# Norm weights beside the loaded features, squares of x in program order and a ScalarE root at the end, in a four-layer decoder trunk

## The chip, the core and the metric

The kernel runs on one core of a Trainium2 chip. Five engines work side by side: PE (TensorE, matrix products; PEld is its loading of weights), DVE (VectorE), ACT (ScalarE), POOL (GpSimd) and SP (SyncE, which here only issues transfers). Each engine takes its own instructions in order; semaphores order them between engines. DMA transfers are issued from the queues of SP, ACT and POOL. The metric is the device time of one execution in microseconds (us), lower being better.

## The reference, cut to what matters

The reference is a decoder trunk of four layers over 256 rows of width 2048, all in float32. Each layer normalizes x, projects it once into the streams of a mixer, four memory query heads and a SiLU gate, and adds an output projection to x. At the end x is normalized once more.

```python
def _rmsnorm(x, g):
    xf = x.astype(jnp.float32)
    y = xf * lax.rsqrt(jnp.mean(xf * xf, axis=-1, keepdims=True) + EPS)
    return (y * g.astype(jnp.float32)).astype(x.dtype)

mem_n = _rmsnorm(mem, mem_norm)
for i in range(DEPTH):
    h = _rmsnorm(x, norm_in[i])
    ...                                   # mixer i % 3, memory attention on mem_n @ w_mem_kv[i]
    y = jnp.concatenate([self_out, mem_out], axis=-1) * jax.nn.silu(gate)
    x = x + y @ w_out[i]
return _rmsnorm(x, final_norm)
```

## The kernel before, in words

**Products in two parts.** Every large product is made from a high and a low part of both operands: ACT copies a float32 tile into a rounded tile (`wh`, L60), DVE subtracts to get the rest (`wl`, L69), and PE runs three products per pair (L265 to L267 for row-wise products, L285 and L289 for column-wise ones). Weights stream from HBM into the tile `wr` (five buffers) by SP's queue; `wh` and `wl` have three buffers each.

**The opening.** `memory()` projects the normalized memory for all four layers (eight steps, each one row-wise product of 16 weight tiles and two column-wise ones). The memory's features (the transposed memory, laid out on the host) come in four tiles `ft` of four 128x256 pieces each, two pieces to a transfer (L88). `weighted_parts` (L193) multiplies a piece by its norm weight, a column of `gvec`, and splits it into the high part (ACT, L60) and the low part (DVE, L198) of `mT`. `gvec` holds all norm weights that are used by feature; ACT's queue loads it as its first transfer (L78). In the very first product the weight tiles come one by one, and a function `each(k)` (L371), called behind the k-th weight tile's transfer, issues the next features behind odd k. PE runs some small products on a tile of ones (L102) while it waits.

**Features of x.** From the second of the eight steps on, a generator `first_chunk(c)` (L322) is run beside the products, once for each quarter of x's features. It issues two loads of `ft` (L326) and two loads of the rows of x (L112), lets six calls of `other_work` go by, makes the four weighted pieces one a call, and then traces two squares-and-sums of the rows of x (L339, the helper's line is L203), one a call. Behind the last quarter, `finish` turns the eight sums into the row scales. The sums are read only by `finish`.

**Who sets the order.** A planner orders each engine's instructions when the program is built: it plays the program against a model of times and lets what is ready go first, by program order among the ready. `keep_in_program_order(i)` adds one edge: i goes behind the instruction that was traced just before it on the same engine. The weighted copies of ACT and the early transfers carry such edges; the squares of x do not. Small tiles come from pools by width: all `[P, 2]` scratch tiles (`mn`, `sm`, `ms`, `rc`, `sd`, `se`, `sa` of the softmaxes, the temporaries of the row scales, and `warm`, on which ACT runs one Exp at the start) share six buffers, and a buffer is free again when its tile's last use is over.

**The late constants.** `late_constants()` (L114) and `bias_table` (L128) load small constants by POOL's queue at the end of the first memory step: `caus`, `cos`, `sin`, `nsink`, then `oh`, `rb` and `mk`, from which PE makes a bias table (L136).

**The end.** `last_out` (L963) makes the last output projection. Its column groups end one after the other; for each, DVE adds the sums to x (L973), ACT squares and sums the new x (L203), and DVE multiplies x by the final norm weight (L978). `share` (L992) gathers the mean of squares, times -1/2; `rsqrt_of` (L994) takes the root by an integer first guess and three Newton steps, seven small DVE instructions (L997, L1002, L1004); `write` (L1008) scales the row tile by pieces on DVE and ACT and stores them. The second row tile is last: its last 256 columns end the program.

Of the kernel before, what the change touches and what calls it, by code (L numbers as in the profile page):

```python
# [8 lines left out]
F32 = mybir.dt.float32  # L9
# [22 lines left out]
def kernel(ctx: ExitStack, tc: tile.TileContext, a: dict, out: bass.AP,  # L32
# [20 lines left out]
    def f32(ap):  # L53
        return ap.bitcast(F32)
# [23 lines left out]
    tc.keep_in_program_order(nc.scalar.dma_start(gvec, a["l_norms"]))  # L78

    class Features:  # L80

        def __init__(self, src, c):
            self.q = act.tile([P, 4, S], F32, name="ft", tag="pq", bufs=PQ)
            self.src = src[:, 4 * c:4 * c + 4, :]

        def load(self, h):
            tc.keep_in_program_order(
                nc.sync.dma_start(self.q[:, 2 * h:2 * h + 2, :], self.src[:, 2 * h:2 * h + 2, :]))  # L88

    mft = [Features(a["l_mem"], c) for c in range(4)]  # L90
    mft[0].load(0)
# [22 lines left out]
    def late_constants():  # L114
        tc.keep_in_program_order(nc.gpsimd.dma_start(caus, a["c_caus"]))
        tc.keep_in_program_order(nc.gpsimd.dma_start(cos, a["c_cos"].rearrange("(t p) d -> p t d", p=P)))
        tc.keep_in_program_order(nc.gpsimd.dma_start(sin, a["c_sin"].rearrange("(t p) d -> p t d", p=P)))
        sk = a["c_sinks"]
        tc.keep_in_program_order(nc.gpsimd.dma_start(
            nsink, bass.AP(tensor=sk.tensor, offset=sk.offset, ap=[[0, P], [1, 32]])))  # L120
        nc.vector.tensor_scalar(nsink, nsink, -1.0, None, op0=OP.mult)
# [71 lines left out]
    def weighted_parts(dst, src, k, gcol):  # L193


        g = gvec[:, gcol + k:gcol + k + 1]
        copy_act(dst[:, 0, k, :], src[:, k, :], scale=g)
        nc.vector.scalar_tensor_tensor(dst[:, 1, k, :], src[:, k, :], g, f32(dst)[:, 0, k, :],  # L198
                                       op0=OP.mult, op1=OP.subtract)

    def square_sum(col, src):
        junk = tmp("junk")
        return nc.scalar.activation(junk[:, :src.shape[-1]], src, AF.Square, accum_out=col).ins  # L203
# [104 lines left out]
    class Norm:  # L308
# [13 lines left out]
        def first_chunk(self, c):  # L322

            ft = Features(a["l_x"], c)
            for h in range(2):
                ft.load(h)  # L326
            first_rows(c)
            for _ in range(12):
                yield True
            q = act.tile([P, 2, 4, S], F32R, name="xT", tag="xT", bufs=4)  # L330
            self.at.append(q)
            for k in range(4):
                pinned.append(c)
                weighted_parts(q, ft.q, k, 64 + c * 4)
                pinned.pop()
                yield True
                yield True
            for t in range(2):
                square_sum(self.ss[:, t * 4 + c:t * 4 + c + 1], x[t][:, c * 512:(c + 1) * 512])  # L339
                yield True  # L340
                yield True
            if c == 3:
                self.finish()
# [20 lines left out]
    def memory():  # L364
# [6 lines left out]
        def each(k):  # L371

            if k % 2 and k < 15:
                mft[(k + 1) // 4].load((k + 1) // 2 % 2)
            if k == 15:
                tc.keep_in_program_order(nc.sync.dma_start(ident, a["c_ident"]))
                nc.vector.tensor_copy(identr, ident)

        def prepare(k):
            c = k // 4  # L380
            weighted_parts(mT[c], mft[c].q, k % 4, c * 4)
# [581 lines left out]
    def last_out(w, part, y):  # L963
# [7 lines left out]
        def add(c0, n, t, acc, col):  # L971
            xs = x[t][:, c0:c0 + n]
            inst = nc.vector.tensor_add(xs, xs, acc)  # L973
            return inst.ins, square_sum(f4[:, t * 5 + col:t * 5 + col + 1], xs)
# [19 lines left out]
        def rsqrt_of(v):  # L994

            i1 = small("fj", 1, I32)
            nc.vector.tensor_scalar(i1, v.bitcast(I32), -0.5, float(0x5F3759DF - (1 << 22) - (1 << 30)),  # L997
                                    op0=OP.mult, op1=OP.add)
            r = i1.bitcast(F32)
            for it in range(3):  # L1000
                u = small("fu", 1)
                nc.vector.scalar_tensor_tensor(u, r, v, r, op0=OP.mult, op1=OP.mult)  # L1002
                r2 = small("fy", 1)
                inst = nc.vector.scalar_tensor_tensor(r2, u, 1.5, r, op0=OP.add, op1=OP.mult)  # L1004
                r = r2
            return r, inst
# [41 lines left out]
        v0 = small("fv", 1)  # L1048
        share(v0, f4[:, 3:4], early[0])
        r, inst = rsqrt_of(v0)  # L1050
# [6 lines left out]
        v1, v2 = small("fv", 1), small("fv", 1)  # L1057
# [3 lines left out]
        share(v2, f4[:, 9:10], v1)  # L1061
        weigh(nc.vector, 1536 + S, S, 1)
        r, inst = rsqrt_of(v2)
# [97 lines left out]
def _laid_out(inputs):  # L1161

    import numpy as np

    def features(v):
        return np.asarray(v)[0].T.reshape(D // P, P, S).transpose(1, 0, 2)
    norms = np.zeros((P, P), np.float32)
    for name, o in (("mem_norm", 0), ("a_q_norm", 32), ("a_kv_norm", 56), ("norm_in", 64)):
        v = np.asarray(inputs[name]).reshape(-1, P)
        norms[o:o + len(v)] = v  # L1170
    return {"l_x": features(inputs["x"]), "l_mem": features(inputs["mem"]), "l_norms": norms.T}
# [27 lines left out]
```

## Time and profile before

| | |
|---|---|
| median of 3 runs | 2589.91 us (2589.48 to 2590.26) |
| the profiled execution | 2588.94 us, span 2587.2 us, granted TensorE clock 0.999 |
| PE busy | 2573.5 us (99% of the span) |
| DVE, ACT, POOL busy | 1878.8, 1619.6, 86.8 us (73%, 63%, 3%) |
| moved by DMA | 520.02 MB, mean 201 GB/s |

The span runs from the first to the last instruction. In rows of the timeline the first number is the start in us from the span's start, the second the duration; a bracket at the end gives the idle time of the engine before the row and what ended it. "PEq", "SPq" and the like are an engine's sequencer, which issues transfers and waits. In lists of waits, the numbers are the total in us, how often, and the longest. A row of a group gives its count, and behind the bar its busy time in us and the mean of one in ns. In rows of transfers the last number is the time from issue to landing. A product row's duration is modelled, and back-to-back products overlap; the step from one start to the next is the cost of one.

### The profile page before, as it was taken

The page shows a single profiled execution, that of the slowest core. Times are in us where ns is not written, and L with a number is a line of the kernel's source. Part 1 is how long each engine was busy: PE and PEld are TensorE (multiplying, and loading weights), DVE is VectorE, ACT ScalarE, POOL GpSimd, SP SyncE. Part 2 cuts the span into 40 slices and gives each one's busy share as a digit, 9 for nine tenths or more (in the row PEclk, how much of TensorE's full clock was granted, in tenths as well). Part 3 has the DMA queues.
Part 4 walks back from the last instruction along what each step waited for, and adds up shares of the span by engine and source line. Part 5 has one row for each costly group of instructions (what it writes and reads, how often), then busy time and mean ns, then how long its engine had stood idle before and what let it go on. Part 6 is the DMA issues. An engine that isn't in the chain of part 4 may idle for free.

```text
span 2587.2 us, 41766 instructions
## 1 busy us (share of the span) xinstructions
PE 2573.5 (99%) x14050; PEld 2214.7 (86%) x14050; DVE 1878.8 (73%) x4145; ACT 1619.6 (63%) x3446; POOL 86.8 (3%) x159
## 2 busy tenths in 40 slices
PE   9999999999999999999999999999999999999998
PEld 8888898888888888888888888888888888888887
DVE  6666667677776686877778776777778767777666
ACT  6556556556656566667666666676666655665654
POOL 1000000000000010000000000000000000000000
PEclk9999999999999999999999999999999999999999
DMA  9887777666677668566656575555655877666664
GB/s 309 255 260 255 241 215 234 182 169 194 190 201 203 198 214 249 167 202 188 187 166 199 169 224 171 172 175 183 195 156 148 239 205 197 192 192 183 209 176 175
DMA packets 459128, 520.02 MB, mean 201 GB/s; under 512 B 69488, under 2 KB 352640, under 8 KB 457248
## 3 DMA queue, kind: packets, MB, share of 16 engines
q1 hardware_dynamic: 441600, 449.72, 59.0%
q0 software_dynamic: 16736, 66.65, 7.9%
q8 instruction: 110, 1.80, 0.3%
q14 instruction: 106, 0.87, 0.1%
q10 hardware_dynamic: 576, 0.98, 0.1%
HBM read 494.10 MB, written 35.75 MB: 205 GB/s over the span
## 4 chain that ended last, share of the span: by engine, by line
PE 91%; DVE 0%; ACT 0%; issue 0%; ACTq 0%; DVEq 0%
PE acc_g L285 14%; PE acc_g L289 7%; PE acc_wo L265 7%; PE acc_wo L266 7%; PE acc_wo L267 7%; PE acc_mq L285 5%; PE acc_cq L285 3%; PE acc_qn L285 3%; PE acc_mq L289 2%; PE acc_mk L285 2%; PE acc_q L266 2%; PE acc_q L267 2%; PE acc_q L265 2%; PE acc_cq L289 2%; PE acc_qn L289 2%; PE ptp L487 1%
## 5 line engine op out<-in xcount | busy, mean ns | idle before, releaser
L69 DVE TENSOR_TENSOR wl<-wr,wh 128x512 fp32r<-128x512 f32 (+2 forms) x1720 | 1160.8, 678 | 620.1 <-ACT wh L60 599.1
L60 ACT ACTIVATE wh<-wr 128x512 fp32r<-128x512 f32 (+2 forms) x1720 | 1065.2, 621 | 797.7 <-PE acc_g L285 173.4
L285 PE MATMUL acc_g<-xT,wh 128*128 128x512 f32 x1536 | 486.8, 396 | 0.0
L289 PEld LDWEIGHTS acc_g<-xT,wl 128*128 128x128 f32 x1536 | 284.5, 188 | 60.5
L289 PE MATMUL acc_g<-xT,wl 128*128 128x256 f32 x1536 | 310.1, 280 | 0.0
L266 PE MATMUL acc_wo<-wl,y 128*128 128x512 f32 x752 | 297.3, 395 | 0.2 <-DVE wl L69 0.2
L267 PE MATMUL acc_wo<-wh,y 128*128 128x512 f32 x752 | 291.8, 390 | 0.0
L285 PEld LDWEIGHTS acc_g<-xT,wh 128*128 128x128 f32 x1536 | 238.3, 189 | 4.5
L265 PE MATMUL acc_wo<-wh,y 128*128 128x512 f32 x752 | 235.7, 392 | 0.1
L266 PEld LDWEIGHTS acc_wo<-wl,y 128*128 128x128 f32 x752 | 141.3, 188 | 27.7 <-DVE wl L69 0.6
L267 PEld LDWEIGHTS acc_wo<-wh,y 128*128 128x128 f32 x752 | 141.3, 188 | 27.3
L265 PEld LDWEIGHTS acc_wo<-wh,y 128*128 128x128 f32 x752 | 139.3, 188 | 28.7 <-ACT y L60 1.0
L285 PE MATMUL acc_mq<-xT,wh 128*128 128x512 f32 x512 | 161.6, 396 | 0.0
L285 PE MATMUL acc_mk<-mT,wh 128*128 128x512 f32 x512 | 161.5, 396 | 0.0
L1112 DVE TENSOR_TENSOR x<-x,acc_wo 128x512 f32<-128x512 f32 x184 | 121.2, 682 | 4.4 <-PE acc_wo L267 4.3
L285 PE MATMUL acc_qn<-cT,wh 128*128 128x512 f32 x384 | 121.3, 397 | 0.0
L285 PE MATMUL acc_cq<-xT,wh 128*128 128x512 f32 x384 | 120.9, 396 | 0.0
L289 PEld LDWEIGHTS acc_mk<-mT,wl 128*128 128x128 f32 x512 | 96.1, 188 | 22.8 <-DVE wl L69 0.4
L289 PEld LDWEIGHTS acc_mq<-xT,wl 128*128 128x128 f32 x512 | 93.9, 188 | 20.1
L289 PE MATMUL acc_mq<-xT,wl 128*128 128x256 f32 x512 | 103.1, 282 | 0.0
L266 PE MATMUL acc_q<-wl,xT 128*128 128x512 f32 x256 | 101.2, 395 | 0.0
L289 PE MATMUL acc_mk<-mT,wl 128*128 128x256 f32 x512 | 101.1, 278 | 0.0
(325 smaller groups left out, 4340.3 us busy)
## 6 DMA issues: line engine op xcount, KB each, us to landing
wr<-in_w_out_dram SPq DMA_DIRECT2D x188, 512.0 KB, 3.7
wr<-in_w_in_a_dram SPq DMA_DIRECT2D x176, 512.0 KB, 4.1
wr<-in_w_mem_kv_dram SPq DMA_DIRECT2D x120, 512.0 KB, 4.8
wr<-in_w_in_b_dram SPq DMA_DIRECT2D x112, 512.0 KB, 3.7
wr<-in_w_in_c_dram SPq DMA_DIRECT2D x104, 512.0 KB, 3.6
wr<-in_w_uq_dram SPq DMA_DIRECT2D x192, 128.0 KB, 3.1
wr<-in_w_uq_dram SPq DMA_DIRECT2D x48, 256.0 KB, 3.8
tab<-flat POOLq DMA_DIRECT2D x8, 1536.0 KB, 9.4
```

Source lines behind the costliest of these rows:

```text
L60: inst = nc.scalar.activation(o, i, AF.Copy, scale=scale)
L69: nc.vector.tensor_sub(lo, src, f32(hi))
L265: nc.tensor.matmul(acc[t][:, :n], xh, wh[:, :n], start=first, stop=False)
L266: nc.tensor.matmul(acc[t][:, :n], xh, wl[:, :n], start=False, stop=False)
L267: nc.tensor.matmul(acc[t][:, :n], xl, wh[:, :n], start=False, stop=last)
L285: nc.tensor.matmul(acc[j], wh[:, o:o + P], q[:, :, kt % 4, :], start=kt == 0, stop=False)
L289: nc.tensor.matmul(acc[j][:, 0, :], wl[:, o:o + P], q[:, 0, kt % 4, :], start=False, stop=kt == kts - 1)
L487: nc.tensor.transpose(tp[:, i * P:(i + 1) * P], es[b][:, k * P:(k + 1) * P], ident)
L1112: nc.vector.tensor_add(xs, xs, acc[t])
```

## The change

- The host lays out the features with the norm weight of each feature as a 257th column, so the tile `ft` becomes 4 x 257 columns and the weight is read from there; `gvec` no longer holds the memory's weights, and its load moves from the head of ACT's queue to the head of `late_constants` on POOL's.
- The first feature tile's first two pieces come in two transfers: the first alone, the second behind the first weight tile's transfer.
- The squares of x in `first_chunk` are kept in program order.
- `rsqrt_of` takes the root with ACT's Sqrt, DVE's reciprocal and one Newton step. A Sqrt on the tile `warm` is traced ahead of the last column groups.

```diff
     gvec = cst.tile([P, P], F32, name="gvec")
-    tc.keep_in_program_order(nc.scalar.dma_start(gvec, a["l_norms"]))
...
-            self.q = act.tile([P, 4, S], F32, name="ft", tag="pq", bufs=PQ)
+            self.q = act.tile([P, 4, S + 1], F32, name="ft", tag="pq", bufs=PQ)
...
-        def load(self, h):
-            tc.keep_in_program_order(
-                nc.sync.dma_start(self.q[:, 2 * h:2 * h + 2, :], self.src[:, 2 * h:2 * h + 2, :]))
+        def load(self, k0, n=2):
+            tc.keep_in_program_order(nc.sync.dma_start(self.q[:, k0:k0 + n, :], self.src[:, k0:k0 + n, :]))
...
-    mft[0].load(0)
+    mft[0].load(0, 1)
...
     def late_constants():
+        tc.keep_in_program_order(nc.gpsimd.dma_start(gvec, a["l_norms"]))
         tc.keep_in_program_order(nc.gpsimd.dma_start(caus, a["c_caus"]))
...
-    def weighted_parts(dst, src, k, gcol):
-        g = gvec[:, gcol + k:gcol + k + 1]
-        copy_act(dst[:, 0, k, :], src[:, k, :], scale=g)
-        nc.vector.scalar_tensor_tensor(dst[:, 1, k, :], src[:, k, :], g, f32(dst)[:, 0, k, :],
+    def weighted_parts(dst, src, k):
+        g = src[:, k, S:S + 1]
+        copy_act(dst[:, 0, k, :], src[:, k, :S], scale=g)
+        nc.vector.scalar_tensor_tensor(dst[:, 1, k, :], src[:, k, :S], g, f32(dst)[:, 0, k, :],
                                        op0=OP.mult, op1=OP.subtract)
...
             for t in range(2):
-                square_sum(self.ss[:, t * 4 + c:t * 4 + c + 1], x[t][:, c * 512:(c + 1) * 512])
+                tc.keep_in_program_order(
+                    square_sum(self.ss[:, t * 4 + c:t * 4 + c + 1], x[t][:, c * 512:(c + 1) * 512]))
                 yield True
                 yield True
...
         def each(k):
+            if k == 0:
+                mft[0].load(1, 1)
             if k % 2 and k < 15:
-                mft[(k + 1) // 4].load((k + 1) // 2 % 2)
+                mft[(k + 1) // 4].load((k + 1) % 4)
...
-        def rsqrt_of(v):
-            i1 = small("fj", 1, I32)
-            nc.vector.tensor_scalar(i1, v.bitcast(I32), -0.5, float(0x5F3759DF - (1 << 22) - (1 << 30)),
-                                    op0=OP.mult, op1=OP.add)
-            r = i1.bitcast(F32)
-            for it in range(3):
-                u = small("fu", 1)
-                nc.vector.scalar_tensor_tensor(u, r, v, r, op0=OP.mult, op1=OP.mult)
-                r2 = small("fy", 1)
-                inst = nc.vector.scalar_tensor_tensor(r2, u, 1.5, r, op0=OP.add, op1=OP.mult)
-                r = r2
-            return r, inst
+        def rsqrt_of(col, rest):
+            e = small("fd", 1)
+            nc.vector.tensor_scalar(e, rest, -2.0, None, op0=OP.mult)
+            v = small("fv", 1)
+            share(v, col, rest)
+            q = small("fq", 1)
+            nc.scalar.activation(q, col, AF.Sqrt, bias=e, scale=1.0 / D)
+            r = small("fr", 1)
+            nc.vector.reciprocal(r, q)
+            u = small("fu", 1)
+            nc.vector.scalar_tensor_tensor(u, r, v, r, op0=OP.mult, op1=OP.mult)
+            r2 = small("fy", 1)
+            return r2, nc.vector.scalar_tensor_tensor(r2, u, 1.5, r, op0=OP.add, op1=OP.mult)
...
             for t in range(2):
                 add(c * 512, 512, t, acc[t], c)
+
+        tc.keep_in_program_order(nc.scalar.activation(warm, warm, AF.Sqrt))
         acc = [ps.tile([P, 512], F32, name="acc_wo2", tag="acc", bufs=4) for c in range(5)]
...
-        v0 = small("fv", 1)
-        share(v0, f4[:, 3:4], early[0])
-        r, inst = rsqrt_of(v0)
+        r, inst = rsqrt_of(f4[:, 3:4], early[0])
...
-        v1, v2 = small("fv", 1), small("fv", 1)
+        v1 = small("fv", 1)
         share(v1, f4[:, 8:9], early[1])
...
-        share(v2, f4[:, 9:10], v1)
         weigh(nc.vector, 1536 + S, S, 1)
-        r, inst = rsqrt_of(v2)
+        r, inst = rsqrt_of(f4[:, 9:10], v1)
```

More of the change, by code (lines that the diff above doesn't have):

```diff
@@ L202, in square_sum @@
         junk = tmp("junk")
-        return nc.scalar.activation(junk[:, :src.shape[-1]], src, AF.Square, accum_out=col).ins
+        return nc.scalar.activation(junk[:, :src.shape[-1]], src, AF.Square, accum_out=col)
     def stage(w, k0, m, cols, each=None):
@@ L325, in first_chunk @@
             for h in range(2):
-                ft.load(h)
+                ft.load(2 * h)
             first_rows(c)
@@ L333, in first_chunk @@
                 pinned.append(c)
-                weighted_parts(q, ft.q, k, 64 + c * 4)
+                weighted_parts(q, ft.q, k)
                 pinned.pop()
@@ L380, in prepare @@
             c = k // 4
-            weighted_parts(mT[c], mft[c].q, k % 4, c * 4)
+            weighted_parts(mT[c], mft[c].q, k % 4)
         def memory_rows(c):
@@ L973, in add @@
             inst = nc.vector.tensor_add(xs, xs, acc)
-            return inst.ins, square_sum(f4[:, t * 5 + col:t * 5 + col + 1], xs)
+            return inst.ins, square_sum(f4[:, t * 5 + col:t * 5 + col + 1], xs).ins
         def weigh(engine, c0, n, t):
@@ L1163, in _laid_out, with features @@
     import numpy as np
-    def features(v):
-        return np.asarray(v)[0].T.reshape(D // P, P, S).transpose(1, 0, 2)
+    def features(v, g):
+        beside = np.concatenate([np.asarray(v)[0].T, np.asarray(g).reshape(-1)[:D, None]], 1)
+        return beside.reshape(D // P, P, S + 1).transpose(1, 0, 2)
     norms = np.zeros((P, P), np.float32)
-    for name, o in (("mem_norm", 0), ("a_q_norm", 32), ("a_kv_norm", 56), ("norm_in", 64)):
+    for name, o in (("a_q_norm", 32), ("a_kv_norm", 56), ("norm_in", 64)):
         v = np.asarray(inputs[name]).reshape(-1, P)
         norms[o:o + len(v)] = v
-    return {"l_x": features(inputs["x"]), "l_mem": features(inputs["mem"]), "l_norms": norms.T}
+    return {"l_x": features(inputs["x"], inputs["norm_in"]),
+            "l_mem": features(inputs["mem"], inputs["mem_norm"]), "l_norms": norms.T}
 _INS = ["x", "mem", "final_norm", "rel_bias", "w_in_a", "w_uq",
```

## The prediction

> **What bounds it now.** I read the page's head and its chain first, then the list of what PE waited for, then the timeline around each of those waits, and last the end. The chain is the work that ended last, followed back.
>
> ```profile
> span 2587.2 us, 41766 instructions
> ...
> PE 91%; DVE 0%; ACT 0%; issue 0%; ACTq 0%; DVEq 0%
> ```
>
> ```profile
> PE acc_mv L265 <- ACT wh L60: 2.5, 2, 1.2
> PE wu L102 <- DVE ones L98: 1.1, 1, 1.1
> PE o L950 <- DVE pT L69: 0.3, 1, 0.3
> ```
>
> PE is the bound nearly from end to end: in 2587 us its waits for other engines come to two stops of 1.2 us behind ACT's `wh` (the opening, and one later); the warm-up on `ones` lies ahead of the first, and the longest after that is 0.3 us. So an edit pays only where it starts PE earlier, takes the second stop away, or shortens what follows the last product. The change touches all three.
>
> **The opening.** The fences give the timeline, the rate of all transfers in slices of 1 us from 0 to 40 us, and the first transfers.
>
> ```profile
> 4.92 0.51 ACT L60 ACTIVATE mT<-ft,gvec 128x256 fp32r<-128x256 f32 x1 [2.24 <-DMA gvec<-in_l_norms_dram]
> ...
> 5.45 0.63 ACT L60 ACTIVATE wh<-wr 128x512 fp32r<-128x512 f32 x1
> ...
> 6.13 0.73 PE L265 MATMUL acc_mv<-wh,mT 128*128 128x512 f32 x2 [1.24 <-ACT wh L60]
> ...
> 8.18 0.63 ACT L60 ACTIVATE wh<-wr 128x512 fp32r<-128x512 f32 x1 [0.34 <-DMA wr<-in_w_mem_kv_dram]
> ...
> 8.84 0.69 DVE L69 TENSOR_TENSOR wl<-wr,wh 128x512 fp32r<-128x512 f32 x1 [0.48 <-ACT wh L60]
> ...
> 9.71 0.40 PE L266 MATMUL acc_mv<-wl,mT 128*128 128x512 f32 x1
> ```
>
> ```profile
> GB/s 0 29 165 268 348 322 336 332 397 383 397 404 393 389 383 377 385 387 393 375 372 352 371 372 359 365 359 366 369 359 353 352 339 345 343 309 343 202 110 362
> ```
>
> ```profile
> ft<-in_l_mem_dram SPq DMA_DIRECT2D x1, 256.0 KB, 4.0
> wr<-in_w_mem_kv_dram SPq DMA_DIRECT2D x1, 256.0 KB, 4.2
> gvec<-in_l_norms_dram ACTq DMA_DIRECT2D x1, 64.0 KB, 4.2
> ```
>
> `gvec`, issued at 0.73, lands at 4.9 and ends ACT's wait; the features (issued at 0.74) lay there at 4.7. But the first weight tile, issued at 1.17, lands only at 5.4, just as ACT is through with its first piece, so taking the wait for `gvec` away gives nothing by itself: the weight tile would be late next. What helps is that less lies ahead of that tile: 128 KB of features (the second piece now follows it) and the 64 KB of `gvec`, 192 KB in all. The rate row shows some 335 GB/s at 4 to 8 us, so the tile lands about 0.59 us earlier, near 4.8. The first piece is then ready too: even if its transfer took 4.0 us as the whole did, `mT` ends at 5.25, and at half the size it should land clearly sooner; I take 0.59.
>
> That is not kept. Behind the second weight tile the bytes ahead are the old ones without `gvec`, 64 KB or 0.20 us less. The third weight tile's landing let ACT go at 8.18, its `wl` ended at 8.84 + 0.69 = 9.53, and PE used it at 9.71: 0.18 us of slack. So PE can be at most 0.18 + 0.20 = 0.38 us earlier at that point. Value: -0.38 us. Ends: -0.59 if the flow is smoother without the second queue; +0.34 if issue and not bandwidth sets the landing, for the extra transfer on SP's queue pushes each following one back by an issue (0.52, half of the 1.04 for the two x transfers below, less the slack of 0.18).
>
> The Trainium skill speaks against the wider rows: "DMA: Bandwidth & Descriptors", section "How a descriptor splits into AXI transactions", says that a transfer row which does not start on a 256-byte boundary is fetched from the boundary below, and the extra bytes cost beats. A row of 257 columns puts most starts off that boundary; at an estimated 4 extra beats on 64, the 512 KB of features ahead of the third tile would act like 32 KB more, 0.10 us, and the whole sum below would be -2.86 instead of -2.96 us. No row of this case has such a start, so the trace does not say.
>
> `gvec` on POOL's queue goes ahead of the late constants, of which PE waits for `rb`:
>
> ```profile
> 60.45 0.51 POOL L132 DMA_DIRECT2D rb<-in_rel_bias_dram  x1
> ```
>
> ```profile
> rb<-in_rel_bias_dram POOLq DMA_DIRECT2D x1, 4.0 KB, 5.4
> ```
>
> ```profile
> 68.49 0.83 PE L136 MATMUL pt<-oh,rb 32*32 32x384 f32 x2
> ```
>
> It pushes them back by one issue, about 0.5 us: `rb` lands at 60.45 + 5.4 + 0.5 = 66.4, 2.1 us before PE uses it. Cost nothing; without that cover 0.5 us. `gvec`'s own next readers come in the first layer, behind all eight memory steps.
>
> **The squares.** Only one of the four pairs meets PE:
>
> ```profile
> 187.15 1.04 SPq L112 DMA_DIRECT2D x<-in_x_dram  x2
> ```
>
> ```profile
> 194.74 0.63 ACT L203 ACTIVATE junk<-x 128x512 f32<-128x512 f32 x1 [2.63 <-DMA x<-in_x_dram]
> ...
> 196.01 1.66 ACT L60 ACTIVATE wh<-wr 128x512 fp32r<-128x512 f32 x3
> ```
>
> ```profile
> 195.08 0.39 PE L267 MATMUL acc_mv<-wh,mT 128*128 128x512 f32 x1
> 196.68 0.73 PE L265 MATMUL acc_mv<-wh,mT 128*128 128x512 f32 x2 [1.21 <-ACT wh L60]
> ...
> 197.74 0.40 PE L267 MATMUL acc_mv<-wh,mT 128*128 128x512 f32 x1
> 197.98 0.40 PE L266 MATMUL acc_mv<-wl,mT 128*128 128x512 f32 x1
> ```
>
> The planner put both squares right behind the issue of x. The rows of x landed 7.6 us after their issue, ACT stood 2.63 us in front of the square, and the `wh` copies queued behind it came too late. PE's step from 197.74 to 197.98 is the usual 0.23; from 195.08 it should have gone on at 195.31 and did at 196.68, 1.37 late, and the three products after that took 1.06 instead of 0.68, another 0.38. Together 1.75 us. In program order the squares come at the 11th and 12th call behind the issue (six go by, four make the pieces); a call comes every two weight tiles of six products at 0.23, 2.7 us, so some 30 us after the issue, in a column-wise product. There ACT's row looks like this:
>
> ```profile
> 258.93 0.63 ACT L60 ACTIVATE wh<-wr 128x512 fp32r<-128x512 f32 x1 [0.76 <-PE acc_mk L285]
> ```
>
> Two squares with their read-outs took from 194.74 to 196.01, 0.64 each, and the hole is 0.76; `wh` has three buffers besides. So eight squares at nothing, value -1.75 us. Behind them only `finish` waits; its chain of small DVE steps moves along into the column-wise product, where it can be split up between `wl`s as before, and its row scales are first used in the first layer. If the cover failed, a `wh` that PE needs at once would come a square's 0.64 late, and the restart's 0.38 on top: +1.0 is the loss end, -1.75 the other.
>
> **The end.** The first fence is the timeline, the second the groups by shape.
>
> ```profile
> 2570.20 0.63 ACT L203 ACTIVATE junk<-x 128x512 f32<-128x512 f32 x1 [1.85 <-DVE x L973]
> ...
> 2580.68 1.12 ACT L60 ACTIVATE xg<-xg,fy 128x384 f32<-128x384 f32 x2 [1.81 <-DVE fy L1004]
> ```
>
> ```profile
> L512 ACT ACTIVATE e<-u,mn 128x256 f32<-128x256 f32 x64 | 32.0, 500 | 3.5 <-DVE mn L507 3.2
> ...
> L512 ACT ACTIVATE e<-u,mn 128x128 f32<-128x128 f32 x64 | 25.1, 393 | 8.8 <-DVE mn L507 8.5
> ```
>
> ```profile
> L530 DVE RECIPROCAL rc<-sm 128x2 f32<-128x2 f32 x64 | 10.2, 159 | 0.1
> ...
> L1002 DVE SCALAR_TENSOR_TENSOR fu<-fy,fv 128x1 f32<-128x1 f32 x4 | 0.9, 218 | 0.2
> ...
> L1004 DVE SCALAR_TENSOR_TENSOR fy<-fu,fy 128x1 f32<-128x1 f32 x4 | 0.6, 156 | 0.1
> ```
>
> ACT's idle time in front of the last scaling, 1.81 us, runs from the read-out of the last sum of squares to the use of the root: small DVE steps, all on the path. New path: Sqrt on ACT, reciprocal, one Newton step. No row has Sqrt; the nearest is the Exp with a bias from a tile: 393 ns at 128 columns, 500 at 256, so 0.84 a column and 0.287 us at one. Then 0.159 + 0.218 + 0.156, together 0.82. The old eight instructions, three pairs of 0.218 + 0.156 and two of about 0.18, are 1.48 of the 1.81, which leaves 0.04 for each gap; four gaps make the new path 0.98 us. `share` (v) runs on DVE beside the Sqrt; the new `e` hangs on sums that are there earlier. Value 0.98 - 1.81 = -0.83 us. Ends: -1.0 (a Sqrt no longer than the reciprocal), -0.5 (0.2 us on each of two hops between engines). The first row tile's root gains the same but is not last: PE's final products end beside it. What follows the root, 2587.2 - 2580.68 = 6.5 us of scaling and stores, stays.
>
> Sqrt needs another function table. The Sqrt on `warm` sits behind the squares that end before the hole of 1.85 us, and one table load took
>
> ```profile
> 1.18 1.28 ACT L95 ACT_TABLE_LOAD   x1 [1.18 <-PEq L1185]
> ```
>
> so it fits with a short Sqrt behind it (1.28 + about 0.2). Cost nothing; if it fell in front of the first row tile's last square instead, 1.5 us there, of which the shorter root gives 0.83 back, and the last row tile does not see it.
>
> **Sum.** -0.38 - 1.75 - 0.83 = -2.96 us. The profiled execution took 2588.94 (1.74 beside its span), so it would take 2586.0; it lies 0.97 under the median of 2589.91, from which I get 2587.0.
>
> **Rivals.** *The held buffer (slower).* `warm` is now used near the end, so one of the six `[P, 2]` buffers is held all along; the layer with sinks (32 heads) uses six such tiles a head. If a head's first tile must wait until the last head's `rc` is read, it loses up to the 0.79 us of those readers.
>
> ```profile
> 1703.14 0.79 ACT L60 ACTIVATE e<-e,rc 128x128 f32<-128x128 f32 x2
> ```
>
> ```profile
> 1706.49 0.34 DVE L507 CUSTOM_DVE_ANT_0 u<-sp,u,nsink 128x128 f32<-128x128 f32 x1
> ```
>
> Four such heads eat the gain; from 11 on (8.7 us) it is slower by over 0.2%, 2595.7, and all 32 give 2612. Against it: in this row a head is through at 1703.93 and the next one's first tile is written 2.6 us later, so heads hardly overlap. *The stop stays.* If late transfers and not the square stop PE near 195, the squares bring nothing: 2588.7. For it: x took 7.6 us. Against it: three `wh` copies ran back to back behind the squares, so their weights had landed. *Another plan.* Any edit makes the planner replay all; PE's waits after the opening are 0.3 us and less but for the one stop, so luck can gain little, while a new stop like the one at 195 costs 1.75 each: two or three give 2590 to 2592.
>
> **Numbers.** Forecast 2587.0: 0.58, own range 2585.3 to 2588.2. Stop stays: 0.14. New stops of the plan: 0.12. Held buffer: 0.11. More gain than all my ends together (0.59 + 1.75 + 1.0 = 3.3) and replanning besides: 0.05. The range 2584.8 to 2592.0 leaves out the held buffer, most of the last case and the worst of the plans. 0.2% is 5.2 us, about what a measurement of this kernel can tell from no change: faster than that 0.05, slower 0.13 (the held buffer, and 0.02 of the plans), within it 0.82.
>
> **What would show it.** Right: ACT's first copy waits for `ft` and PE starts near 5.6; no PE stop near 195 and the squares some 30 us behind the issue of x; one table load near 2568; about 1 us from the last read-out to `xg`. Wrong: PE waits in the attention stages with scratch tiles as the cause, a second table load in the end, or a stop at 195 that now ends on a transfer.

## The result, and the profile after

The changed kernel takes 2619.8 us (median of 4 runs, 2619.12 to 2620.33) against 2589.69 (2589.31 to 2590.26) of the kernel before on the same chip: a ratio of 1.0116, 95% interval 1.0103 to 1.0128. It is 30 us slower, where 3 us less were forecast. The profiled execution took 2620.01 us with a span of 2618.2.

The head of the page of the changed kernel, and the list of what PE waited for (total in us, how often, longest):

```profile
span 2618.2 us, 41763 instructions
...
PE 2606.4 (100%) x14050; PEld 2221.3 (85%) x14050; DVE 1879.8 (72%) x4139; ACT 1623.6 (62%) x3450; POOL 87.3 (3%) x160
...
PEclk9999999999999999999999999999999999999999
...
PE 99%; DVE 0%; DMA 0%; ACT 0%; SPq 0%; issue 0%; ACTq 0%
```

```profile
PE acc_mv L264 <- ACT wh L60: 1.4, 1, 1.4
PE wu L100 <- DVE ones L96: 1.1, 1, 1.1
PE o L952 <- DVE pT L69: 0.3, 1, 0.3
```

PE waits less than before: the stop at 195 us is gone. The number of products is the same, 14,050, and the granted clock is full in every slice. Yet PE's busy time has grown from 2573.5 to 2606.4 us, by 33 us. So no wait was added: the products themselves take longer. A stretch in which PE is never idle shows it. The columns are the stretch, its length, and busy time and number of instructions of each engine; first the kernel before, then the changed one:

```profile
500.00:1000.00 500.00, 500.00 (x2704) 429.22 (x2703) 359.76 (x769) 306.65 (x623) 16.13 (x30) 1.00 0.69 199
```

```profile
500.00:1000.00 500.00, 500.00 (x2672) 425.67 (x2671) 356.43 (x762) 300.69 (x611) 13.77 (x25) 1.00 0.67 192
```

In the same 500 us PE starts 2672 products in place of 2704, 1.2% fewer: just the 1.2% of the whole. Which products are they? The groups by line, with busy time and the mean of one in ns, for the kernel before and then for the changed kernel (a product's modelled length runs past the start of the next, but a difference of lengths is a difference of steps):

```profile
L285 PE MATMUL acc_g<-xT,wh 128*128 128x512 f32 x1536 | 486.8, 396 | 0.0
L289 PE MATMUL acc_g<-xT,wl 128*128 128x256 f32 x1536 | 310.1, 280 | 0.0
L266 PE MATMUL acc_wo<-wl,y 128*128 128x512 f32 x752 | 297.3, 395 | 0.2 <-DVE wl L69 0.2
L267 PE MATMUL acc_wo<-wh,y 128*128 128x512 f32 x752 | 291.8, 390 | 0.0
```

```profile
L284 PE MATMUL acc_g<-xT,wh 128*128 128x512 f32 x1536 | 487.1, 396 | 0.0
L288 PE MATMUL acc_g<-xT,wl 128*128 128x256 f32 x1536 | 314.2, 282 | 0.0
L265 PE MATMUL acc_wo<-wl,y 128*128 128x512 f32 x752 | 300.7, 400 | 0.1
L266 PE MATMUL acc_wo<-wh,y 128*128 128x512 f32 x752 | 295.6, 395 | 0.0
```

Of a product's two operands, one (the moving one) is streamed through PE and the other (the stationary one, a block of 128x128) is loaded ahead of it. Row-wise products (the moving operand is `wh` or `wl`, 512 columns) take 5 ns more each, all over the kernel, in layers that no edit touches. Column-wise ones with 256 moving columns take 2 ns more, those with 2x256 nearly the same. From the start times of all products, row-wise ones take 230.3 ns a step before and 235.6 after (4544 of them), column-wise ones 117.6 and 119.9 (3456 with 256 columns) and 234.2 and 234.5 (3456 with 2x256): 24.1 + 7.9 + 1.0 = 33.0 us. That is the whole loss and the 3 us that the parts of the change were to bring.

What did the edit do to all products at once? It moved their operands. The tile pools lay their tiles one behind another in order of first use. A tile `ft` of 4 x 257 columns has 4112 bytes on a partition, which the pool rounds up to 4128; it had 4096. Five such buffers lie ahead of `mT`, `cT`, the values, `y` and `xT`, so all these start 160 bytes later, while `wr`, `wh` and `wl` lie in a pool ahead of them and stay. The traces hold no addresses; by the sizes of the tiles, `wh`, `wl` and all these tiles start at one place within 256 bytes in the kernel before, and in the changed kernel the activations start 160 bytes past that place. Whether that is the cause, and what about it, the runs had to tell.

The three places that the change was aimed at, in the changed kernel. The opening, ACT and PE:

```profile
3.02 0.51 ACT L60 ACTIVATE mT<-ft 128x256 fp32r<-128x256 f32 x1 [0.79 <-DMA ft<-in_l_mem_dram]
4.49 0.63 ACT L60 ACTIVATE wh<-wr 128x512 fp32r<-128x512 f32 x1 [0.96 <-DMA wr<-in_w_mem_kv_dram]
```

```profile
5.18 0.72 PE L264 MATMUL acc_mv<-wh,mT 128*128 128x512 f32 x2
...
9.90 0.72 PE L264 MATMUL acc_mv<-wh,mT 128*128 128x512 f32 x2 [1.40 <-ACT wh L60]
```

One pair of squares (issue of x on SP's queue, then the squares on ACT), and the end on ACT:

```profile
191.03 0.90 SPq L110 DMA_DIRECT2D x<-in_x_dram  x2
```

```profile
214.41 0.62 ACT L202 ACTIVATE junk<-x 128x512 f32<-128x512 f32 x1
...
216.79 0.62 ACT L202 ACTIVATE junk<-x 128x512 f32<-128x512 f32 x1
```

```profile
2600.08 1.28 ACT L1036 ACT_TABLE_LOAD   x1
2601.38 0.20 ACT L1036 ACTIVATE warm<-warm 128x2 f32<-128x2 f32 x1
...
2610.29 0.19 ACT L202 ACTIVATION_READ_ACCUMULATOR junk<-x 128x1 f32 x1
2610.80 0.30 ACT L1004 ACTIVATE fq<-fs,fd 128x1 f32<-128x1 f32 x1 [0.33 <-DVE fd L1000]
2611.77 1.12 ACT L60 ACTIVATE xg<-xg,fy 128x384 f32<-128x384 f32 x2 [0.68 <-DVE fy L1010]
```

PE starts 0.95 us earlier than before (5.18 against 6.13) and then waits for the third weight tile; the squares come 23 us behind the issue of x and meet nobody; there is one table load in the end, and the root takes 1.29 us from the end of the read-out to the scaling. None of the three can hold 30 us.

### The profile page after: what moved, and what is told of

Read it like the earlier page. It is cut to its first block, busy times and chain, and to the rows that moved or that the text cites. A ratio compares the mean times of both kernels' runs of the same rounds, so it can differ in the third digit from the quotient of the medians.

```text
span 2618.2 us, 41763 instructions
## 1 busy us (share of the span) xinstructions
PE 2606.4 (100%) x14050; PEld 2221.3 (85%) x14050; DVE 1879.8 (72%) x4139; ACT 1623.6 (62%) x3450; POOL 87.3 (3%) x160
## 4 chain that ended last, share of the span: by engine, by line
PE 99%; DVE 0%; DMA 0%; ACT 0%; SPq 0%; issue 0%; ACTq 0%
PE acc_g L284 14%; PE acc_g L288 7%; PE acc_wo L264 7%; PE acc_wo L265 7%; PE acc_wo L266 7%; PE acc_mq L284 5%; PE acc_mk L284 5%; PE acc_cq L284 3%; PE acc_qn L284 3%; PE acc_mq L288 2%; PE acc_mk L288 2%; PE acc_q L266 2%; PE acc_q L265 2%; PE acc_q L264 2%; PE acc_mv L265 2%; PE acc_mv L266 2%
## 5 line engine op out<-in xcount | busy, mean ns | idle before, releaser
L266 PE MATMUL acc_wo<-wh,y 128*128 128x512 f32 x752 | 295.6, 395 | 0.0
L264 PE MATMUL acc_wo<-wh,y 128*128 128x512 f32 x752 | 239.2, 396 | 0.1
L1115 DVE TENSOR_TENSOR x<-x,acc_wo 128x512 f32<-128x512 f32 x184 | 121.0, 681 | 5.2 <-PE acc_wo L266 4.8
```

The lines of the kernel that those rows point to most:

```text
L264: nc.tensor.matmul(acc[t][:, :n], xh, wh[:, :n], start=first, stop=False)
L266: nc.tensor.matmul(acc[t][:, :n], xl, wh[:, :n], start=False, stop=last)
L1115: nc.vector.tensor_add(xs, xs, acc[t])
```

## The experiments

The theory: TensorE's step depends on where its two operands start, by the distance between the tile that moves and the tile that is loaded. Rivals: each operand's own start counts; or the parts of the change cost (wider rows in DRAM, pinned squares, Sqrt, another order).

### The place alone, and the change at another place

Run e1: the changed kernel with a wider feature tile, so that all tiles start at multiples of 64 bytes again; the distance becomes 128 bytes.

```diff
-            self.q = act.tile([P, 4, S + 1], F32, name="ft", tag="pq", bufs=PQ)
+            self.q = act.tile([P, 4, S + 8], F32, name="ft", tag="pq", bufs=PQ)[:, :, :S + 1]
```

> The changed kernel with its feature tiles 264 columns wide in place of 257 (column 257 to 263 unused, the transfers unchanged), so that each is 4224 bytes and every tile behind them starts at a multiple of 64 bytes again as in the kernel before. If the 30 us come from where the tiles start (512-column matmuls on wh and wl went from steps of 227 ns to 232, 256-column ones on xT from 116 to 118, all over the kernel), those steps return to 227 and 116 and the time is that of the three parts of the change alone, by the trace of after: opening -0.8 (PE starts at 5.18 in place of 6.13, but stops 1.56 at 8.11), stop at 195 gone -1.75, root -0.8: 2586 to 2588. If they come from the parts themselves (rows of 257 columns in DRAM, pinned squares, Sqrt, another order by the planner), the steps stay at 232 and the time at 2619.

Runs e2 to e4: the kernel before with an unused tile, and nothing else.

```diff
+    nc.gpsimd.memset(act.tile([P, 8], F32, name="pad_act"), 0.0)     # e2: activations only
...
+    nc.gpsimd.memset(wp.tile([P, 8], F32, name="pad_wp"), 0.0)       # e3: weights, and all behind them
...
+    nc.gpsimd.memset(wp.tile([P, 8], F32, name="pad_wp"), 0.0)       # e4: both pads, so the weights
+    nc.gpsimd.memset(act.tile([P, 8], F32, name="pad_act"), 0.0)     # move by 32 and the rest by 64
```

> The kernel before with nothing but a 32-byte tile at the head of the pool of activations (one memset on GpSimd writes it), so that xT, mT, cT, y, the keys and values start 32 bytes past a multiple of 64, and pT, hl and e, which lay there before, start at a multiple of 64. Place theory: all of the loss comes back, 4460 matmuls of 512 columns times 5.3 ns and 3456 of 256 columns times 2.3 ns plus 3456 of 2x256 times 0.4 ns = 33 us, so 2621 to 2624. Rival, that the loss belongs to the parts of the change: 2589 to 2591.

> The kernel before with the 32-byte tile at the head of the pool of weights, so that wr, wh, wl are shifted by 32 bytes as well as everything behind them. Moving and stationary operand of nearly every projection then start at the same offset within 64 bytes again, but both at 32. If what costs is a difference between the two operands of a matmul: steps of 227 and 116, 2589 to 2592. If each operand that starts off a multiple of 64 costs by itself: at least the 2622 of the run with the activations alone, more with the weights' share on top (up to 2650). If the parts of the change cost: 2590.

> The kernel before with a 32-byte tile at the head of the pool of weights and another at the head of the pool of activations: wr, wh, wl start at 32 within 64 bytes, all others as before. If a difference between the operands costs: as with the activations shifted alone, 2620 to 2624. If the stationary operand alone costs (the 512-column steps on wh and wl have y, xT or mT as stationary): those 4460 go back to 227, and the 6912 with wh or wl stationary and xT moving rise instead by some 5 ns each, 2615 to 2630, which shows in which groups have the longer steps. If the moving one alone: the 4460 on wh and wl rise by 2 to 5 ns, 2600 to 2612, and those on xT stay at 233 and 116.

Run e5: the changed kernel with an unused tile behind the feature buffers, which moves the activations to 512 bytes from their old place. Run e8: the same with 96 bytes, so 256 from the old place. Run e12: the kernel before with the activations at exactly the changed kernel's addresses.

```diff
     mft = [Features(a["l_mem"], c) for c in range(4)]
+    nc.gpsimd.memset(act.tile([P, 88], F32, name="pad"), 0.0)        # e5; e8 has 24 columns
...
+    nc.gpsimd.memset(act.tile([P, 40], F32, name="pad_act"), 0.0)    # e12: ahead of all, in the kernel before
```

> The changed kernel with an unused tile of 352 bytes behind its five feature buffers: these take 5 x 32 = 160 bytes more than before, so that mT, cT, y, xT and the values are now shifted by 512 bytes against the kernel before, and their distance to wh and wl is a multiple of 512 bytes again; only the keys and queries that share the feature buffers stay off (distances of 0, 32, 64, 96, 128). Multiples of 64 bytes between the operands were not enough (distance 128: steps of 232 and 117 ns, 2608.9 us). Theory, that the distance between the operands of a matmul must be a multiple of 512 bytes (the size of a 128-column weight block): steps of 227 and 116 return and the three parts of the change show what they are worth: 2586 to 2588. Rival, that a still larger period counts (1024 or 2048 bytes, the size of a wh buffer): 2600 to 2620. Rival, that the widened feature buffers or the parts themselves cost what is left: 2605 to 2620 with steps of 227.

> The changed kernel with an unused tile of 96 bytes behind the feature buffers, so that mT, cT, y and xT are shifted by 256 bytes (not 512) against the kernel before. TensorE alone showed the same steps at 0, 256, 512 and 4096 bytes (227 and 115) and longer ones between. If 256 bytes is the period in the whole kernel too: steps of 227 and 116, 2586.2 to 2587.5, as with 512. If the kernel needs 512: steps of 230 and more, 2600 to 2620.

> The kernel before with nothing but an unused tile of 160 bytes at the head of the pool of activations: xT, mT, cT, y, the values and the scratch tiles lie at exactly the addresses that they have in the changed kernel, and no part of the change is in it. With 32 bytes the loss was 20 us, the changed kernel (160 bytes) lies 32.8 us above its version with 256 bytes (2619.8 against 2587.0). If the place alone makes the whole difference: 2589.5 + 32.8 = 2622.3, between 2620.5 and 2624. If part of it needs the change itself (the feature buffers' own uneven starts, the wider rows): about the 2609 of the run with 32 bytes, up to 2618.

Measured, with the mean steps worked out from the start times of all products (the distance is that of the activations' start to the weights' start, within 256 bytes):

| kernel | distance, bytes | row-wise, ns | 2x256, ns | 256, ns | median, us | ratio to before, 95% |
|---|---|---|---|---|---|---|
| before | 0 | 230.3 | 234.2 | 117.6 | 2589.69 | |
| changed | 160 | 235.6 | 234.5 | 119.9 | 2619.8 | 1.0116 (1.0103 to 1.0128) |
| e12: before, activations moved | 160 | 235.6 | 234.5 | 119.9 | 2621.66 | 1.0124 (1.0107 to 1.0141) |
| e2: before, activations moved | 32 | 235.7 | 230.8 | 120.2 | 2609.48 | 1.0077 (1.0064 to 1.0091) |
| e4: before, both moved | 32 | 235.2 | 230.6 | 120.2 | 2608.94 | 1.0076 (1.0061 to 1.0092) |
| e3: before, all moved by 32 | 0 | 230.5 | 234.2 | 117.6 | 2589.5 | 1.0000 (0.9991 to 1.0009) |
| e1: changed, tiles at multiples of 64 | 128 | 234.6 | 232.6 | 119.6 | 2608.94 | 1.0075 (1.0063 to 1.0088) |
| e5: changed, moved by 512 | 0 | 230.2 | 234.0 | 117.7 | 2586.94 | 0.9988 (0.9979 to 0.9998) |
| e8: changed, moved by 256 | 0 | 230.3 | 234.2 | 117.6 | 2586.96 | 0.9991 (0.9982 to 0.9999) |

The groups of e2, of e3 and of e12, in the same columns as above:

```profile
L267 PE MATMUL acc_wo<-wl,y 128*128 128x512 f32 x752 | 300.8, 400 | 0.1
L268 PE MATMUL acc_wo<-wh,y 128*128 128x512 f32 x752 | 295.6, 395 | 0.0
```

```profile
L267 PE MATMUL acc_wo<-wl,y 128*128 128x512 f32 x752 | 297.2, 395 | 0.1
L268 PE MATMUL acc_wo<-wh,y 128*128 128x512 f32 x752 | 291.9, 390 | 0.0
```

```profile
L267 PE MATMUL acc_wo<-wl,y 128*128 128x512 f32 x752 | 300.6, 400 | 0.1
L268 PE MATMUL acc_wo<-wh,y 128*128 128x512 f32 x752 | 295.8, 395 | 0.0
```

Three things follow. First, the place alone makes the loss: e12 has no part of the change in it and shows the changed kernel's three steps to 0.1 ns. The unused tile and its memset cost nothing by themselves, since e3 has them too. Second, it is the distance that counts and not the start of either tile: with all tiles 32 bytes further (e3) nothing is lost, and e2 and e4, which put the tiles at other places but at one distance, agree within 0.6 us. Third, my first guess of what distance is harmless, a multiple of 64 bytes, was wrong: e1 at 128 bytes loses 22 us against e8. At 256 and at 512 bytes nothing is lost, and the changed kernel takes 2587.

The expectations for e2, 2621 to 2624, and for e4, 2620 to 2624, missed by over 11 us since they took the steps of distance 160 for those of 32: there the products with 2x256 columns gain 3.4 ns. The size depends on the distance, form by form. The time of e4 lies in the 2600 to 2612 that its expectation gave for the moving operand alone, but its steps speak against that: the column-wise ones did not stay, and in e3 the moving operand moved as well and no step changed by more than 0.2 ns.

### TensorE by itself

Run e6 leaves out everything but products on tiles of zeros: for each distance 24 in the row-wise order and 32 in the column-wise one.

```diff
+        for d in steps:
+            q = y[:, d:d + 2048].rearrange("p (v k c) -> p v k c", v=2, k=4)
...
+                    for n, (m, s) in enumerate(((wh, xh), (wl, xh), (wh, xl))):
+                        pin(nc.tensor.matmul(acc[t], s, m, start=k + n == 0, stop=k + n == 5))
```

> Everything of the computation is left out (the output is zeros); what is left is TensorE alone: for 25 distances between the start of the weights' tile and that of the activations' tile (0 to 4096 bytes) 24 matmuls in the order of the row-wise product (512 moving columns of w, 128x128 of y stationary) and 32 in the order of the column-wise one (2x256 and 256 moving columns of y, w stationary), with no other engine running. Theory, that the moving stream and the loading of the next stationary block meet in SBUF: steps of 227 and 116 ns at 0, 512, 1024, 2048 and 4096 bytes and 230 to 236 and 118 to 120 at the others, the column-wise 512 the other way round (233 at 0, 229 off it). Rival, that it takes the other engines' reading and writing of the weight tiles to lose the time: one step for all distances, 227 and 113 to 116.

The timeline of PE in this run; the accumulators are named by the distance in bytes. A set's time is from its start to the start of the next one:

```profile
31.19 5.61 PE L55 MATMUL rows0B<-w,y 128*128 128x512 f32 x24
36.64 0.62 PE L60 MATMUL cols0B<-y,w 128*128 128x512 f32 x2
...
64.66 5.76 PE L55 MATMUL rows32B<-w,y 128*128 128x512 f32 x24
70.26 0.63 PE L60 MATMUL cols32B<-y,w 128*128 128x512 f32 x2
...
298.66 5.61 PE L55 MATMUL rows4096B<-w,y 128*128 128x512 f32 x24
304.11 0.61 PE L60 MATMUL cols4096B<-y,w 128*128 128x512 f32 x2
```

24 row-wise products take 5.45 us at 0 and at 4096 bytes and 5.60 at 32: steps of 227.1 and 233.3 ns. Means of the steps in ns, from the start times, for 12 of the 25 distances:

| distance, bytes | 0 | 8 | 32 | 64 | 96 | 128 | 160 | 192 | 224 | 256 | 288 | 512 |
|---|---|---|---|---|---|---|---|---|---|---|---|---|
| row-wise | 227.1 | 230.9 | 233.3 | 232.9 | 234.2 | 232.4 | 233.8 | 228.7 | 233.3 | 229.4 | 233.2 | 227.4 |
| 2x256 | 232.5 | 235.2 | 229.1 | 230.2 | 231.9 | 232.3 | 233.4 | 231.2 | 233.4 | 232.6 | 228.4 | 232.5 |
| 256 | 115.4 | 121.7 | 118.3 | 116.5 | 121.0 | 118.3 | 118.1 | 116.0 | 118.3 | 115.3 | 118.7 | 115.4 |

So no other engine is needed, and the rival is out. The pattern comes back after 256 bytes, not the 512 of the expectation (32 as 288). At 256 itself one set gave 229.4 row-wise and a repeat 227.1, so a single set can be 2 ns off. 8 bytes are enough to lose 4 ns. The kernel's losses are somewhat smaller: at 160 bytes the row-wise step rises by 6.7 here and by 5.3 in the kernel.

Run e7, products alone as well, asked which operand's distance counts.

```diff
+        wh, wl = w[:, h:h + 512], w[:, 576 + l:][:, :512]        # part 1: h, l = 0, 8, ... 56 columns
...
+            s = y[:, b + d0:b + d0 + P] if n % 2 == 0 else y[:, b + d1:b + d1 + P]        # part 2
```

> TensorE alone again, the computation left out (the output is zeros). First part: the column-wise order with the two stationary tiles shifted one by one against the moving tile, wh by 0 to 224 bytes and wl by 0 to 224 bytes in steps of 32 (64 sets of 32 matmuls). In the first run of TensorE alone the step of 2x256 columns was shortest at 32 bytes (229.1 ns against 232.5 at 0) and that of 256 columns at 0 (115.4 against 118.3). If each step depends on the distance of the block that is loaded while it streams, there are pairs with both short: 344 to 346 ns for the two together against 347.9 at 0/0. If it depends on its own block alone, the pair wh 32, wl 0 gives 229.1 + 115.4 = 344.5 exactly. If the moving tile's own start is what counts, all 64 pairs give 348. Second part: 512 moving columns, even matmuls with a stationary block at one distance (0, 32 or 128 bytes) and odd ones at another. If the block that is loaded during the stream counts, the step that starts at an even matmul is long (232 to 234) where the odd one's distance is 32 or 128, whatever its own; if its own counts, the other way round.

None of the three expectations of the first part held. `wh` at 32 and `wl` at 0 gave 350.3 ns for the pair of column-wise products, not 344.5 or 348; over all 64 pairs it lay between 346.3 and 356.5, against 348.1 at 0/0. That pair was the wrong one to look at, though: e6 moved the activations and e7 moves the weights, so a distance of 32 there is a shift by 224 here. The pair 224 and 0 gave 346.3, the least of all. But with `wh` left at 224 the step of 2x256 columns runs from 229.4 to 235.8 as `wl` is moved, so its own block alone does not set it. In the second part, with one block at 0 and the next at 0 both steps were 227 (227.6 and 227.1); at 0 and 32 they were 232.2 and 237.3, at 32 and 0 231.0 and 229.0, at 32 and 32 235.0 and 231.7 (the five pairs with 128 bytes lie between 229.1 and 233.7). An odd block lengthens the step that starts at the even one and its own, so it is neither the streaming product's own block alone nor the next one alone. How the two streams meet inside the memory stays open. For use it is enough: of all that was tried, row-wise products are shortest where all starts agree.

### The parts, at a harmless place

Two runs on the base of e8. Run e10 takes the pin off the squares; run e11 has the old root and no Sqrt.

```diff
-                tc.keep_in_program_order(
-                    square_sum(self.ss[:, t * 4 + c:t * 4 + c + 1], x[t][:, c * 512:(c + 1) * 512]))
+                square_sum(self.ss[:, t * 4 + c:t * 4 + c + 1], x[t][:, c * 512:(c + 1) * 512])
```

> As the run with 96 bytes, but the squares of x are left to the planner again. If the pinned squares are what took the stop at 195 us away (1.75 us in the sum of the prediction): the stop is back and the time 2588.3 to 2589.0. If the other parts moved the stop away already (the plan is another one with the earlier opening): 2586.5 to 2587.3 and no stop.

> As the run with 96 bytes, but the last root is computed on VectorE with three Newton steps as in the kernel before, and the Sqrt on warm is gone. If the new root is worth what the trace says (ACT's idle time in front of the last scaling 1.81 us with the old root): 2587.4 to 2588.0. If the table load or the two engines' exchange eats it: 2586.5 to 2587.2.

e10: 2587.97 us (2587.09 to 2589.06), 1.0 above e8's 2586.96 (2586.70 to 2587.57). A stop is back, at another place: PE waits for `wh` twice now, once in the opening and once at 152 us, and from 76 to 214 us it falls 1.6 us behind e8.

```profile
PE acc_mv L265 <- ACT wh L60: 1.2, 2, 0.8
```

ACT in e10 at that place shows the old mechanism, with another quarter of x: the square waits for x, and the `wh` copies come behind it.

```profile
150.98 0.63 ACT L203 ACTIVATE junk<-x 128x512 f32<-128x512 f32 x1 [1.91 <-DMA x<-in_x_dram]
...
152.22 1.66 ACT L60 ACTIVATE wh<-wr 128x512 fp32r<-128x512 f32 x3
```

The median lies below the 2588.3 to 2589.0 that was expected of a stop that is back, and above the range without one.

e11: 2587.82 us (2587.31 to 2588.22), 0.9 above e8. ACT at the end of e11, with the old root, and then of e8, with the new one:

```profile
2577.56 0.19 ACT L203 ACTIVATION_READ_ACCUMULATOR junk<-x 128x1 f32 x1
2579.56 1.12 ACT L60 ACTIVATE xg<-xg,fy 128x384 f32<-128x384 f32 x2 [1.81 <-DVE fy L1007]
```

```profile
2576.98 0.19 ACT L203 ACTIVATION_READ_ACCUMULATOR junk<-x 128x1 f32 x1
2577.49 0.29 ACT L1005 ACTIVATE fq<-fs,fd 128x1 f32<-128x1 f32 x1 [0.33 <-DVE fd L1001]
2578.46 1.12 ACT L60 ACTIVATE xg<-xg,fy 128x384 f32<-128x384 f32 x2 [0.68 <-DVE fy L1011]
```

From the read-out's end to the scaling 1.81 us became 1.29. From the last product to the end of the span it is 9.7 us in e11 (2576.3 to 2586.0) and 9.0 in e8 (2575.9 to 2584.9).

### A better version

Run e9: as e8, and the attention's scratch tiles `pT` and `hl`, 96 bytes off their partners in both kernels, moved by 160.

```diff
+            if i == 0:
+                nc.gpsimd.memset(wk.tile([P, 40], F32, name="padw"), 0.0)
             sq = wk.tile([P, S], F32, name="cqs", tag="sco0", bufs=1)
```

> As the run with 96 bytes, and besides an unused tile of 160 bytes ahead of the attention's scratch tiles, so that pT and hl, which lie 96 bytes off a multiple of 256 from their partners vz, mvr and va in every kernel so far, lie at a distance of 0 too. The 512-column matmuls on pT and vz (95 of them, 238.5 ns) would go to about 232, those of 256 columns on pT (350 of them, 119 ns) to 116: 0.6 + 1.0 us, so 2585.0 to 2586.2 and the first version well below both kernels. Rival: in attention the steps are set by other things (waits, the other operands), no change: 2586.5 to 2587.3.

2585.85 us (2585.12 to 2586.30): 1.1 below e8 and, at a ratio of 0.9985 (0.9976 to 0.9994), the fastest kernel here, 34 us below the changed one. The products on `pT` and `vz`, in e8 and then in e9:

```profile
L953 PE MATMUL o<-pT,vz 128*128 128x512 f32 x96 | 32.5, 399 | 0.4 <-DVE pT L69 0.4
```

```profile
L955 PE MATMUL o<-pT,vz 128*128 128x512 f32 x96 | 32.2, 397 | 0.3 <-DVE pT L69 0.3
```

Their steps fell from 237.6 to 234.4 ns, those on `pT` with 256 columns (`mo` and `o`) by 1.2 and 1.4: some 0.7 us by the counts, as a distance that costs would have it, though less than the 1.6 that was expected. The two traces are 1.6 us apart: besides these 0.7, 0.4 lies in the opening, and the rest is spread over other products without a cause that was found.

## Why the prediction was wrong

**The step that failed** is the sum itself: it had a term for each wait and none for the products. The first part showed that PE is the bound nearly from end to end, and drew from it that an edit pays only where it starts PE earlier, takes the stop away or shortens the end. That left out the other side: with 14,050 products in a row, an edit that lengthens most of them by a few ns costs more than all waits together. The wider rows of `ft` were costed as a transfer; that the tile itself grew and moved everything behind it was no step at all. Measured in place of this zero: +33 us (e12 against before 32.4, changed against e8 32.8). The range, 2584.8 to 2592.0, had no case for it, and the 0.13 for slower stood on other causes.

**The sum of the waits** was nearly right. At a harmless place the same change takes 2586.94 and 2586.96 us, by 2.9 and 2.3 less than the kernel before beside it, where 2.96 and 2587.0 were forecast. That the whole came so near is in part luck: the squares held, the opening shows no gain, and the end is smaller by the trace.

- *Opening, -0.38.* ACT did wait for `ft`, and PE started at 5.0 to 5.3 us in the seven traces with the change (5.5 to 6.1 in the five without), before the 5.6 that was named. That the third weight tile would take the gain back was right, and it took more: it landed at 8.1 to 9.2 us with the change and at 8.2 to 9.4 without, a scatter of 1 us that hides a gain of 0.38. The extra transfer did push that tile's issue back, from 2.58 to 3.06 us, as the loss end of this term assumed. In e5 and e8 the 350th product starts 0.15 and 0.5 us later than in the trace of before, whose third tile was the earliest of those five, and in e3, without the change, 1.46 us later. Nothing shows a gain or a loss. The Trainium skill's rule ("DMA: Bandwidth & Descriptors", "How a descriptor splits into AXI transactions"), by which the sum was -2.86, would change the landing by an estimated 0.10 us; within this scatter no run here shows it.
- *Squares, -1.75.* In the traces of e5 and e8 PE gains 1.8 us on before between its 700th and 1050th product, around the old stop. That size held; the squares came 23 us behind the issue, not 30. Taking the pin off costs 1.0 us by the medians and 1.6 by the trace, but at other places (1.1 at 152 us and 0.5 at 108), so it prices the stops of another plan.
- *End, -0.83.* The term was too large for the root and nearer for the whole: the path fell by 0.52, from 1.81 to 1.29, not to 0.98. The Sqrt lasted 0.29 to 0.30, as estimated, but it stands 0.33 us behind `fd`. Its sums are there earlier, as the prediction says, but DVE takes its work in order, and a multiplication of 0.42 us lies ahead. The other 0.17 came from the first row tile's root, called "not last": its scaling no longer holds up DVE before the last addition to x (0.12 us) and ACT before the last square (0.05), which starts 0.77 us behind the start of the last product in place of 0.94. Together -0.69; by the medians of e11 and e8 -0.86.
- *Rivals.* The held buffer: no wait of PE on scratch tiles appears in any list; it is out. The stop stays: out, it is gone with the pin. Another plan: e10 shows that the planner does put new stops elsewhere, but with the pin none came. One table load, in a hole, as said.

**Two read ports.** The Trainium skill ("SBUF — State Buffer", "Who interferes with whom") gives PE two independent read ports, one for the moving operand and one for loading weights, and names the port pair that DVE shares with GpSimd as the only place of contention. By that rule the steps of e6 would be the same at all distances. For 512 moving columns they are 227.1 ns at 0 and 228.7 to 234.2 from 8 to 224 bytes with PE alone, so here the measurement decides. Whether the two ports meet, or what else makes the difference, no run shows.

## What to carry to other kernels

Where PE is the bound from end to end, compare the steps of its products before and after an edit, ahead of any wait: a busy time that grew with the same number of products and the same clock means longer steps. A tile that changes size moves every tile allocated behind it; look at the addresses, and keep the starts of the tiles that meet in products like these at one place within 256 bytes, with an unused tile where needed. When an edit loses for no reason that can be seen, put nothing but its change of addresses into the old kernel: that run (e12) alone put 32.4 of the 32.8 us down to the place.

## What the runs showed of the hardware

- In run e6 the step of back-to-back products of float32r tiles, each with its own load of 128x128, depends on the distance of the two operands' starts in SBUF: 227.1 ns at 0 and 228.7 to 234.2 at 8 to 224 bytes for 512 moving columns, 115.4 against 116.0 to 121.7 for 256. It repeats after 256 bytes and needs no other engine. For 2x256 columns 0 is not the best: 232.5 at 0, 229.1 at 32 bytes.
- A shift of all operands by 32 bytes changes nothing (e3: 2589.5 us against 2589.59).
- The landing of the third weight tile varied from 8.1 to 9.4 us over the traces of the twelve whole kernels; in the five without the change, which issue it at 2.58 or 2.59 us, from 8.2 to 9.4.
